# Other points in the pace at which a four-layer hybrid kernel streams its modulation weights

## The chip, the cores and the metric

The kernel runs on one core of a Trainium2 chip. The metric is device time in microseconds (us) of one execution, given as the median of several. A core has five engines that work side by side, each through its own instructions in order: TensorE (PE; its weight loads are listed as PEld), VectorE (DVE), ScalarE (ACT), GpSimd (POOL) and SyncE (SP). SP computes nothing here: it issues most of the transfers from memory, in order, and waits for the target buffer of each before it issues it.

## The reference

Four residual layers over 256 tokens of width 2048, batch 1, float32 throughout. Layer `i` first makes three vectors of 2048 from a conditioning vector `c`; the layer kinds are RWKV-7 (layers 0 and 3), gated linear attention (layer 1) and a state-space layer, SSD (layer 2).

```python
c_act = silu(c)
for i in range(4):
    mod = einsum('bd,de->be', c_act, ada_w[i]) + ada_b[i]     # ada_w[i]: 2048 x 6144
    shift, scale, gate = split(mod, 3)
    h = rms_normalize(x, norm_g[i]) * (1 + scale) + shift
    out = (rwkv7_mixer, gla_mixer, ssd_mixer)[i % 3](h, ...)  # projections in, a scan, a projection out
    x = x + gate * out
return rms_normalize(x, final_g)
```

Every `(i, q)` with `q` = 0, 1, 2 (shift, scale, gate) is called a **third** here: 2048 x 2048 weights against one vector. The reference does them ahead of each layer; none of them depends on `x`, so a kernel can do them at any time before they are used.

## The kernel before

**Projections.** `x` is kept as 16 tiles of 128 channels by 256 tokens. A projection takes its weights in **chunks** of up to 128 x 1024 float32 (512 KB). For each chunk, SP loads it into one of the six buffers `raw` (L348), ACT rounds it to `H` (L338), DVE makes the rest `L = raw - H` (L340), and PE multiplies `H` with both parts of the input and `L` with the first (L393). After the matmuls of each chunk, `jobs` (L359) calls `tick` (L395). There are 670 ticks; 36 further chunks (the first part of layer 0's V projection, and the small low-rank weights of layers 0 and 3) have none, so that L338 runs 706 times. Counted by these casts in time order, ticks can be laid over the trace: that is how the stretches of the tables below were cut.

**The stages, in ticks.** Layer 0 (RWKV): the end of V is 1 to 8, K 9 to 40, R 41 to 72, G 73 to 104, the output projection 105 to 144 (in three parts, of four, three and one of the eight head groups). While K is projected, `rwkv_first` works on DVE, ACT, PE and the transfers of SP and POOL for each of eight head groups; it ends in `unit_inverse`, a chain of small DVE steps and transfers through memory. `rwkv_second` does the scan during R and after. Layer 1 (GLA) is 145 to 276, layer 2 (SSD) 277 to 502, in eight groups of 20 ticks with an output projection of 16 ticks after each second group, and layer 3 (RWKV) 503 to 670.

**The thirds.** `ada_third` (L290) does one third in 32 **steps** of a generator: a step loads 512 KB of `ada_w` into a buffer `raw`, the same six as above, by SP (L298), and DVE adds it, multiplied by the entry of `c_act` for each row, to the running sum `adaacc` (L304; ACT does the first of 16, L302). After each 16 steps, eight matmuls of PE (L310, L316), a copy of ACT and an addition of DVE (L317) put the half third into `mod`. The shift and scale of layer 0 are done ahead, in another way, by `ada_group`. Ten thirds are left, in the order (0,2), (1,0), (1,1), (1,2), (2,0) ... (3,2): 320 steps and one that closes the last.

**The pace.** `tick` reads the number of steps due at this tick from `PACE` (L96): ticks and steps, with straight lines between. It takes at most two steps at one tick. It takes none while `hold` is set, which is from the last 256 columns of a layer's output projection until the first projection of the next layer is through. Whoever uses a third calls `ada_need` (L331), which takes all steps that are still missing at once: `norm_parts` (L498) and `scaled` need shift and scale at the start of a layer, and `outproj` (L424) the gate. Steps forced like this are not counted by `tick`, so the generator is ahead by as many from then on.

**The order.** A scheduler in the compiler lays out each engine's order from the order in which the program names the instructions, and moves an instruction forward where it expects its engine to be free. Steps that come after a layer's end in the program can so stand among the last instructions of the layer.

Of the kernel before, what the change touches and what calls it, by code (L numbers as in the profile page):

```python
# [92 lines left out]

RAWC = 1024

PACE = ((0, 60, 78, 150, 319, 530, 660), (0, 0, 16, 96, 234, 292, 320))  # L96

SHARE = (1, 0, 1, 0, 1, 0, 1, 0)

# [30 lines left out]
class Kern:  # L130
# [264 lines left out]
    def tick(self):  # L395

        self.tk += 1
        n = min(int(np.interp(self.tk, *PACE)), self.paced + 2)
        if not self.hold:
# [1072 lines left out]
```

## Time and profile before

| | us |
|---|---|
| median of 3 runs | 2889.27 |
| lowest and highest | 2874.83, 2891.78 |
| the profiled execution | 2887.0 |
| its span, from its first to its last instruction | 2885.0 |

The rows further down are from the profiled execution, whose own time is 2 us over its span and 2 us under the median. An engine's busy time is the union of its instructions; "(x12)" is a count. "PEclk" is TensorE's granted clock as a share of 2.4 GHz, so 0.50 is 1.2 GHz. In a timeline row the bracket at the end is the engine's idle time before the instruction, and what ended it.

### The profile page before, as it was taken

The page shows a single profiled execution, that of the slowest core. Times are in us where ns is not written, and L with a number is a line of the kernel's source. Part 1 is how long each engine was busy: PE and PEld are TensorE (multiplying, and loading weights), DVE is VectorE, ACT ScalarE, POOL GpSimd, SP SyncE. Part 2 cuts the span into 40 slices and gives each one's busy share as a digit, 9 for nine tenths or more (in the row PEclk, how much of TensorE's full clock was granted, in tenths as well). Part 3 has the DMA queues.
Part 4 walks back from the last instruction along what each step waited for, and adds up shares of the span by engine and source line. Part 5 has one row for each costly group of instructions (what it writes and reads, how often), then busy time and mean ns, then how long its engine had stood idle before and what let it go on. Part 6 is the DMA issues. An engine that isn't in the chain of part 4 may idle for free.

```text
span 2885.0 us, 64064 instructions
## 1 busy us (share of the span) xinstructions
PE 2686.2 (93%) x26098; PEld 2505.1 (87%) x26098; DVE 2212.4 (77%) x3918; ACT 1392.8 (48%) x2315; POOL 154.6 (5%) x298
## 2 busy tenths in 40 slices
PE   6899999999987899988998999999889999999997
PEld 4789889887877899987988999999879988988887
DVE  5778777877788888877898788887668897666666
ACT  3475655433335454434544454554457756453333
POOL 0011110101000000000000000000000111010100
PEclk8899999999998999999999999999989999999999
DMA  9866557977677888976784767776557665585543
GB/s 348 308 231 190 176 161 261 347 266 278 207 261 244 293 285 291 324 268 197 277 294 161 242 219 228 224 226 216 167 171 236 230 208 190 178 297 194 207 132 108
DMA packets 239126, 673.68 MB, mean 234 GB/s; under 512 B 72272, under 2 KB 78416, under 8 KB 235760
## 3 DMA queue, kind: packets, MB, share of 16 engines
q1 hardware_dynamic: 217904, 580.84, 60.2%
q0 software_dynamic: 20928, 88.75, 8.5%
q8 instruction: 205, 3.36, 0.5%
q14 instruction: 89, 0.73, 0.1%
HBM read 620.66 MB, written 48.82 MB: 232 GB/s over the span
## 4 chain that ended last, share of the span: by engine, by line
PE 66%; DVE 8%; DMA 8%; issue 3%; ACT 2%; SPq 1%; POOL 0%; DVEq 0%; ACTq 0%; POOLq 0%
PE acc L393 53%; DMA raw<-in_ada_w 3%; DVE L L340 2%; PE g L785 2%; DVE adaacc L304 1%; ACT H L338 1%; PE b L897 1%; DMA raw<-in_gla_w_in 1%; DMA dx<-bd 1%; DMA raw<-in_rwkv_w_in 1%; PE b L866 1%; DMA raw<-in_rwkv_w_out 1%; PE b L873 1%; DMA sp<-yd 1%; PE b L1030 1%
## 5 line engine op out<-in xcount | busy, mean ns | idle before, releaser
L393 PE MATMUL acc<-xs,H 128*128 128x256 f32 x8480 | 1634.4, 291 | 36.5 <-ACT H L338 8.1
L393 PEld LDWEIGHTS acc<-xs,H 128*128 128x128 f32 x8480 | 1362.8, 196 | 69.3 <-ACT H L338 11.4
L393 PE MATMUL acc<-xs,L 128*128 128x256 f32 x4240 | 1230.6, 291 | 17.1 <-DVE L L340 16.2
L338 ACT CAST H<-raw 128x1024 fp32r<-128x1024 f32 (+1 forms) x706 | 718.0, 1018 | 854.9 <-PE acc L393 634.3
L340 DVE TENSOR_TENSOR L<-raw,H 128x1024 fp32r<-128x1024 f32 (+1 forms) x706 | 833.7, 1183 | 248.9 <-ACT H L338 234.0
L393 PEld LDWEIGHTS acc<-xs,L 128*128 128x128 f32 x4240 | 830.8, 196 | 31.1 <-DVE L L340 21.5
L304 DVE SCALAR_TENSOR_TENSOR adaacc<-raw,cact,adaacc 128x1024 f32<-128x1024 f32 x300 | 384.0, 1280 | 132.6 <-DMA raw<-in_ada_w 130.2
L393 PE MATMUL acc<-ys,H 128*128 128x256 f32 x1536 | 293.3, 291 | 12.2 <-DVE ys L409 4.9
L393 PEld LDWEIGHTS acc<-ys,H 128*128 128x128 f32 x1536 | 245.9, 195 | 22.0 <-issue 6.6
L393 PE MATMUL acc<-ys,L 128*128 128x256 f32 x768 | 222.1, 290 | 0.4 <-DVE L L340 0.4
L393 PEld LDWEIGHTS acc<-ys,L 128*128 128x128 f32 x768 | 149.6, 195 | 4.6 <-issue 3.6
L551 ACT ACTIVATE hn<-x,mod,omu 128x256 f32<-128x256 f32 x192 | 113.4, 599 | 1.5 <-DVE x L542 1.2
L431 DVE SCALAR_TENSOR_TENSOR x<-acc,mod,x 128x256 f32<-128x256 f32 x192 | 83.6, 477 | 35.7 <-PE acc L393 35.3
L393 PE MATMUL acc<-H,xs 128*128 128x256 f32 x512 | 97.1, 290 | 1.6 <-ACT vt L1078 1.6
L554 DVE SCALAR_TENSOR_TENSOR xm<-x,par,hn 128x256 f32<-128x256 f32 x192 | 88.6, 476 | 1.4 <-ACT hn L551 0.3
L393 PEld LDWEIGHTS acc<-H,xs 128*128 128x128 f32 x512 | 82.4, 197 | 3.1 <-ACT vt L1078 1.8
L393 PE MATMUL acc<-L,xs 128*128 128x256 f32 x256 | 73.8, 289 | 0.0
L785 PE MATMUL g<-abkp 64*128 64x128 f32 x768 | 65.8, 293 | 4.0 <-DVE G L823 2.7
L408 ACT CAST xs<-xm 128x256 fp32r<-128x256 f32 x128 | 50.9, 400 | 35.4 <-DVE xm L554 33.0
L785 PEld LDWEIGHTS g<-abkp 64*128 64x128 f32 x768 | 52.2, 190 | 15.8 <-issue 8.8
L1284 DVE SCALAR_TENSOR_TENSOR cva<-cvp,hcw,cva 128x256 f32<-128x256 f32 x144 | 64.9, 476 | 0.0
L278 DVE SCALAR_TENSOR_TENSOR adaacc<-raw,cact,adaacc 128x512 f32<-128x512 f32 x56 | 41.9, 748 | 27.5 <-DMA raw<-in_ada_w 23.0
(358 smaller groups left out, 3063.0 us busy)
## 6 DMA issues: line engine op xcount, KB each, us to landing
raw<-in_ada_w SPq DMA_DIRECT2D x384, 512.0 KB, 4.8
raw<-in_rwkv_w_in SPq DMA_DIRECT2D x256, 512.0 KB, 4.7
raw<-in_ssd_w_in SPq DMA_DIRECT2D x128, 512.0 KB, 4.4
raw<-in_gla_w_in SPq DMA_DIRECT2D x96, 512.0 KB, 5.2
raw<-in_ssd_w_out SPq DMA_DIRECT2D x64, 512.0 KB, 4.2
raw<-in_rwkv_w_out SPq DMA_DIRECT2D x48, 512.0 KB, 4.2
abkp<-kd POOLq DMA_DIRECT2D x16, 1024.0 KB, 7.3
raw<-in_gla_w_out SPq DMA_DIRECT2D x32, 512.0 KB, 4.9
```

Of the source, the lines that this page charges most:

```text
L278: nc.vector.scalar_tensor_tensor(out=acc, in0=raw[:, u, :], scalar=self.cact[:, k:k + 1], in1=acc, op0=ALU.mult, op1=ALU.add)
L304: nc.vector.scalar_tensor_tensor(out=acc, in0=raw, scalar=self.cact[:, k:k + 1], in1=acc, op0=ALU.mult, op1=ALU.add)
L338: nc.scalar.copy(out=hi, in_=raw[:, a:a + n])
L340: nc.vector.tensor_tensor(out=lo, in0=raw[:, a:a + n], in1=hi, op=ALU.subtract)
L393: self.nc.tensor.matmul(ps, lhs, rhs, start=first and part == 0 and w is hi, stop=last and w is lo)
L408: nc.scalar.copy(out=t[:, 0, :], in_=src)
L431: nc.vector.scalar_tensor_tensor(out=self.x[:, t, 1:], in0=ps[:, u, :], scalar=gate[:, t:t + 1], in1=self.x[:, t, 1:], op0=ALU.mult, op1=A ...
L551: nc.scalar.activation(t1, x[:, k, 1:], AF.Identity, scale=self.omu[:, col:col + 1], bias=self.mods[(i, 0)][:, k:k + 1])
L554: done[k] = nc.vector.scalar_tensor_tensor(out=xm, in0=x[:, k, 0:T], scalar=self.p("rwkv_mu", col), in1=t1, op0=ALU.mult, op1=ALU.add)
L785: self.nc.tensor.matmul(ps[h][:, n * C:(n + 1) * C], s[r, q, c * C:(c + 1) * C], t[r, q, c * C:(c + 1) * C], start=True, stop=True)
L866: nc.tensor.matmul(ps[r, n * H:(n + 1) * H], G[h][:, q, r], tk[:, 2, q, HS[h]], start=not c, stop=not c or h == 1)
L1284: nc.vector.scalar_tensor_tensor(out=a, in0=src[:, k:k + T], scalar=w[k], in1=a, op0=ALU.mult, op1=ALU.add)
```

## The change

One line: the points of `PACE`. No instruction is added or taken away; the 320 steps, with their loads and sums, come at other ticks.

```diff
-PACE = ((0, 60, 78, 150, 319, 530, 660), (0, 0, 16, 96, 234, 292, 320))
+PACE = ((0, 57, 134, 272, 496, 620), (0, 36, 98, 194, 290, 320))
```

Worked through `tick`, `hold` and `ada_need` by hand, the two lists give these steps (times are those of the kernel before):

| stage | ticks | us of the span | steps before | steps after |
|---|---|---|---|---|
| layer 0, end of V | 1-8 | 180-201 | 0 | 5 |
| layer 0, K | 9-40 | 201-343 | 0 | 20 |
| layer 0, R | 41-72 | 343-498 | 10 | 23 |
| layer 0, G and output, first part | 73-120 | 498-784 | 52 | 38 |
| layer 0, output, other parts | 121-144 | 784-872 | 26 | 18 |
| forced at the start of layer 1 by (1,1) | | 872-890 | 9 | 0 |
| layer 1, decay and head 0 | 145-172 | 890-988 | 25 | 20 |
| layer 1, other heads, first output | 173-260 | 988-1272 | 72 | 61 |
| layer 1, last output | 261-276 | 1272-1345 | 12 | 9 |
| layer 2, groups 0, 1, first part of 2 | 277-330 | 1345-1549 | 40 | 24 |
| forced at the first output of layer 2 by (2,2) | | | 0 | 7 |
| layer 2, first output | 331-346 | 1549-1611 | 4 | 7 |
| layer 2, rest of group 2 to group 7 | 347-486 | 1611-2047 | 38 | 60 |
| layer 2, last output | 487-502 | 2047-2120 | 4 | 5 |
| layer 3 | 503-670 | 2120-2885 | 29 | 24 |

## Rows read from the trace of the kernel before

**Rows 1.** The page, engines: busy us, share of the span, instructions.
```profile
PE 2686.2 (93%) x26098; PEld 2505.1 (87%) x26098; DVE 2212.4 (77%) x3918; ACT 1392.8 (48%) x2315; POOL 154.6 (5%) x298
```

**Rows 2.** The page, costliest groups: busy, mean ns | idle before, releaser.
```profile
L338 ACT CAST H<-raw 128x1024 fp32r<-128x1024 f32 (+1 forms) x706 | 718.0, 1018 | 854.9 <-PE acc L393 634.3
...
L304 DVE SCALAR_TENSOR_TENSOR adaacc<-raw,cact,adaacc 128x1024 f32<-128x1024 f32 x300 | 384.0, 1280 | 132.6 <-DMA raw<-in_ada_w 130.2
```

**Rows 3.** Windows, all engines: stretch, us, busy by engine, PEclk, DMA share, GB/s.
```profile
201.00:343.00 142.00, 136.39 (x1508) 129.81 (x1506) 115.95 (x253) 90.84 (x178) 15.32 (x28) 0.98 0.59 188
343.00:498.00 155.00, 145.77 (x2128) 138.19 (x2129) 108.80 (x206) 84.05 (x158) 15.78 (x31) 0.92 0.64 203
498.00:784.00 286.00, 270.34 (x2900) 242.31 (x2899) 223.58 (x379) 100.76 (x164) 30.71 (x57) 0.95 0.80 278
784.00:872.00 88.00, 74.60 (x617) 64.51 (x615) 69.54 (x111) 30.36 (x54) 1.07 (x2) 0.96 0.74 257
...
890.00:988.00 98.00, 90.81 (x664) 83.69 (x665) 83.56 (x114) 55.72 (x86) 0.52 (x1) 0.93 0.71 245
988.00:1272.00 284.00, 282.38 (x2322) 269.07 (x2321) 230.28 (x287) 129.22 (x180) 0.00 (x0) 1.00 0.84 298
1272.00:1345.00 73.00, 64.98 (x467) 58.20 (x465) 51.22 (x73) 27.58 (x46) 0.00 (x0) 0.91 0.71 238
1345.00:1549.00 204.00, 181.46 (x1441) 172.68 (x1441) 180.13 (x335) 105.36 (x161) 2.72 (x5) 0.92 0.73 253
1549.00:1611.00 62.00, 55.09 (x449) 52.86 (x448) 47.23 (x92) 25.12 (x34) 0.53 (x1) 0.92 0.57 187
1611.00:2047.00 436.00, 435.63 (x3693) 428.00 (x3692) 357.15 (x633) 221.01 (x312) 1.59 (x3) 1.00 0.69 223
2047.00:2120.00 73.00, 64.21 (x472) 56.23 (x471) 40.81 (x70) 25.49 (x41) 4.34 (x6) 0.91 0.51 169
2243.00:2390.00 147.00, 137.17 (x1363) 129.51 (x1362) 123.32 (x263) 93.58 (x183) 14.92 (x26) 0.95 0.67 219
...
2538.00:2808.00 270.00, 267.00 (x3136) 241.19 (x3135) 175.80 (x337) 100.84 (x168) 31.79 (x59) 0.99 0.60 206
2808.00:2869.00 61.00, 60.13 (x509) 54.92 (x507) 40.74 (x80) 26.92 (x46) 0.00 (x0) 1.00 0.32 100
```

**Rows 4.** Windows of L304 alone: stretch, us, DVE busy (count), PEclk, DMA share, GB/s.
```profile
498.00:784.00 286.00, 61.49 (x48) 0.95 0.80 278
784.00:872.00 88.00, 30.73 (x25) 0.96 0.74 257
...
988.00:1272.00 284.00, 86.84 (x68) 1.00 0.84 298
...
1345.00:1549.00 204.00, 44.79 (x35) 0.92 0.73 253
...
1611.00:2047.00 436.00, 44.88 (x35) 1.00 0.69 223
...
2243.00:2390.00 147.00, 7.68 (x6) 0.95 0.67 219
...
2538.00:2808.00 270.00, 5.10 (x4) 0.99 0.60 206
```

**Rows 5.** Timeline of PE at the ends of layers 0 and 1.
```profile
872.34 0.61 PE L471 MATMUL nb<-cst,hn 128*128 128x1 f32 x4 [0.46 <-ACT hn L468]
882.97 1.08 PE L310 MATMUL mx<-adaacc,cst 128*32 128x256 f32 x8 [10.03 <-DVE rsr L1049]
...
889.83 0.58 PE L393 MATMUL b<-xs,H 128*128 128x256 f32 x1 [1.52 <-ACT xs L411]
...
1348.47 0.61 PE L471 MATMUL b<-cst,hn 128*128 128x1 f32 x4 [0.41 <-ACT hn L468]
...
1358.85 0.80 PE L393 MATMUL acc<-xs,H 128*128 128x256 f32 x2 [1.52 <-ACT xs L411]
```

**Rows 6.** Timeline of SP's issues at the end of layer 0.
```profile
862.42 11.14 SPq L298 DMA_DIRECT2D raw<-in_ada_w  x8
```

## The prediction, made before the run

> **What bounds the kernel now.** First comes the page's line of engines: PE is busy for 93% of the span, DVE for 77% [rows 1], so that the whole is near PE's work and no average tells what a step costs. I therefore read the windows, cut at the stages. Two regimes stand side by side. In the middle of layer 1 PE has no gap to speak of (282.4 of 284 us) though 68 steps' sums (L304) lie in it; in the later groups of layer 2 it is the same (435.6 of 436 us), with 35 of them [rows 3, 4]. There a step more or less is covered by PE. At the start of layer 2, though, DVE is busy for 180.1 of 204 us, 0.883, while PE has 23 us of gaps and a granted clock of 0.92 [rows 3]: what ends last there is DVE. I take **0.883** as the most that DVE reaches in a stretch of this kernel that it bounds. Last, the timeline at the layers' ends: at the end of layer 0, PE has done the norm's last small matmul at 872.3 and begins layer 1 at 889.8, 17.5 us later; at the end of layer 1 the same takes 10.4 us (1348.5 to 1358.9) [rows 5]. At the end of layer 0 SP issues eight loads of modulation weights one after another, in 11.1 us [rows 6]: these are the nine steps forced by the third (1,1), as counted in the table of the change. PE's long wait there ends with DVE's reciprocal root (L1049), which shares DVE with their sums.
>
> **The change, part by part.** Nothing is removed; each moved step takes along 512 KB on SP's queue and on the six buffers, and 1.28 us of DVE [rows 2]. Gains are negative; steps are those of the table.
>
> *Layer 0, K: 20 steps more.* DVE is busy for 115.95 of 142 us without one [rows 3]. With 20 x 1.28 = 25.6 us it would need 141.6 us; at 0.883 that takes 160 us, **+18**. Layer 3's K carries 6 sums and takes 147 us [rows 3, 4]: 5 us for 6, by which 20 cost 17. I take **+17**. Ends: 0 (141.6 fits in 142 if DVE had no gap) and +26 (each at its full length). The load that waits for a buffer has behind it on SP's queue the next chunk's load and the transfers of `unit_inverse`, for whose landing DVE waits: this is what could push it to the upper end. The Trainium skill (Perfetto Trace Analysis, section Identifying the Most-Contended Engine) would have us look for the engine with the highest occupancy and optimize it first; in K that is PE, with 136.4 against DVE's 116.0 us, and read so, K's term would be 0 and the sum 17 lower. The start of layer 2 speaks against leaning on the order of the two: there they are within 1.4 us of each other and both have gaps.
>
> *End of V, 5 more.* Layers 0 and 3 give a price for mild loads: G with the first part of the output takes 286 us with 48 sums and 270 us with 4, 16 / 44 = 0.36 us each [rows 3, 4]. For 5: **+2**; ends 0 and +6 (full length).
>
> *R, 13 more.* DVE has 108.8 of 155 us; with 16.6 more it is at 0.81 [rows 3], as in the middle of layer 1 where PE has no gaps. So the mild price, 13 x 0.36 = **+5**; ends 0 and +17.
>
> *G and first output, 14 fewer.* The same price, **-5**; ends 0 and -10 (twice that).
>
> *Output, other parts: 8 fewer.* This stage takes 88 us with 25 sums in layer 0 and 61 us with none in layer 3 [rows 3, 4], 27 / 25 = 1.08 us each: 8 x 1.08 = 9. By DVE: 40.74 us without sums, 18 x 1.28 = 23.0 more, over 0.883: 72 us, a gain of 16. I take **-11**, nearer to the measured price; ends -4 and -20.
>
> *The forced nine, gone.* The new pace has 104 steps there, seven over what (1,1) needs, so the end of layer 0 becomes like that of layer 1 now, where later steps also stand among the norm's instructions: 10.4 for 17.5, **-7**. Ends 0 and -10. What is late next is the norm's own chain of DVE, PE and ACT.
>
> *Layer 1.* Decay and head 0 have 5 steps fewer, in 98 us with DVE at 83.6, 0.85 [rows 3], near the ceiling. A sum there is worth up to 1.28 / 0.883 = 1.45 us, so at most 7; **-4**. The other heads lose 11 under a full PE: **0**. The last output has 3 fewer; it takes 73 us, and so does layer 2's last output, with next to no steps [rows 3]: **0**, at best -5.
>
> *Layer 2, start: 16 fewer.* DVE would need 180.1 - 20.5 = 159.6 us, at 0.883 181 us, a gain of 23. At K's price, 0.83 us each, it is 13. PE alone needs 181.5 us less what its clock cost it. I take **-15**, nearer to the measured price; ends -5 and -24.
>
> *Layer 2, first output: 3 more and 7 forced.* In the new pace, tick 330 has 218 steps and the gate (2,2) needs 225, so `ada_need` takes 7 at once ahead of the first output projection. Eight such loads held SP's queue for 11.1 us [rows 6]; queued behind these 7 are the output's own chunks, and on DVE the sums stand ahead of group 2's work. PE has the chunks already loaded, and may write two accumulators before it needs the gate. Nothing in the trace of before shows how much of this is covered, as the forced steps there met an empty PE. Ends: -5 (the stage, now 62 us, has gaps of 7 us [rows 3] that could close by a lighter DVE before it) and +14 (7/8 of 11.1, and 3 sums at 1.28). I take **+7**, half of the upper end.
>
> *Rest of layer 2: 22 more.* DVE goes from 357.2 to 385 of 436 us, which is 0.883 itself, under a PE without gaps. Ends 0 and +28. The middle of layer 1 has 0.24 sums per us at no cost; here they go from 0.08 (35 in 436) to 0.13 [rows 3, 4]; I take **+5**, below the mild price (8).
>
> *Last output of layer 2, and layer 3: 4 fewer in all, spread.* **0**, within 3 either way.
>
> Sum: 17 + 2 + 5 - 5 - 11 - 7 - 4 - 15 + 7 + 5 = -6, on 2887.0: 2881. The profiled execution lies 2 us under the median, so 2883 beside 2889.3; I give **2882**. The pace moves the price of DVE's sums from four places to four others, and little is left over. One per cent (29 us) is about what a measurement of this kernel can tell from no change.
>
> **Rivals.**
> *(A) Slower: K and R don't take more DVE work.* If the chains of `unit_inverse` and the scan set DVE's share there, added sums lengthen the stages at today's shares: K 141.6 / 0.817 = 173, +31; R 125.4 / 0.702 = 179, +24; V's end +9 (6.4 / 0.702). That is 64 instead of 24, the sum +34: **2921**. For: DVE waits for transfers of the inverse in K, and these share SP's queue. Against: layer 3's K has 0.84 with 6 sums. It is slower than before once V, K and R together cost over 30 us.
> *(B) Faster: sums are free where DVE has gaps and cost the ceiling's price where it has none.* K +7 (at 0.95), V, R and the rest of layer 2 at 0; the two relieved stages at their DVE figures, -16 and -23. Sum: 7 - 5 - 16 - 7 - 4 - 23 + 7 = -41: **2846**. For: full PE in layers 1 and 2 under 68 and 35 sums. Against: the measured 5 us for 6 sums in layer 3's K. The Trainium skill (Perfetto Trace Analysis, section Optimization Strategy) says that where the contended engine changes over time, interleaving the regimes may improve performance; that is this case, and no run here has shown it yet.
> *(C) The change doesn't do what it says:* the third (2,2) is not complete in time, and its forced steps cost what those of layer 0 did, a stop of 17.5 us instead of 7. Sum +4: **2891**. For: the count. Against: PE has work waiting there.
>
> **How the numbers follow.** The forecast has 0.50, A 0.15, B 0.22, C 0.13. The terms' ends, taken as independent, put some 28 us either way on the forecast, and B and A lie beyond; a range from **2850 to 2915** leaves out about half of A and B each. Faster by over 1% (under 2860): three quarters of B and a little of the forecast, 0.20. Slower by over 1% (over 2918): over half of A and a little of the forecast, 0.12. Within 1%: 0.68.
>
> **What would show it.** Right: K near 160 us with about 20 sums and DVE near 0.88; the stop at the end of layer 0 near 10 us; layer 2's start some 15 us shorter with about 19 sums; seven loads in a row on SP before layer 2's first output, with a gap of PE of some us behind them. Wrong: K at 173 or more (A), K under 150 and the later groups of layer 2 without gaps (B), PE standing for 15 us or more at the first output of layer 2 (C). The prediction fails as a whole if the compiler's new order opens gaps in places where the number of steps didn't change.

## The result, and the profile after

| | before | after |
|---|---|---|
| median | 2883.82 us (6 runs) | 2908.19 us (6 runs, 2900.42 to 2909.74) |
| ratio after / before | | 1.0081, 95% interval 1.0054 to 1.0107 |
| the profiled execution | 2887.0 us | 2903.33 us |
| its span | 2885.0 us | 2901.2 us |

The kernel became 24 us slower. The time lies inside the range of 2850 to 2915, but the forecast, 2882, had a small gain. The page of the changed kernel first: its engines, its chain that ended last (shares by engine) and its group of the sums, which answer to [rows 1, 2]. The row by itself below is the chain of the kernel before.

```profile
PE 2690.8 (93%) x26098; PEld 2505.2 (86%) x26098; DVE 2212.6 (76%) x3918; ACT 1396.8 (48%) x2315; POOL 154.3 (5%) x298
...
PE 59%; DMA 17%; DVE 15%; issue 5%; ACT 2%; SPq 1%; DVEq 0%; POOL 0%; ACTq 0%; POOLq 0%
...
L304 DVE SCALAR_TENSOR_TENSOR adaacc<-raw,cact,adaacc 128x1024 f32<-128x1024 f32 x300 | 384.2, 1281 | 228.7 <-DMA raw<-in_ada_w 224.8
```

```profile
PE 66%; DVE 8%; DMA 8%; issue 3%; ACT 2%; SPq 1%; POOL 0%; DVEq 0%; ACTq 0%; POOLq 0%
```

Every busy time is as it was. What has changed is the end of the sums' row: DVE stood idle 228.7 us ahead of them, against 132.6 [rows 2], nearly all of it for their own loads; and in the chain DMA and DVE have taken shares from PE. The windows tell where, against [rows 3, 4]; first all engines (us, busy by engine PE, PEld, DVE, ACT, POOL, PEclk, DMA share, GB/s), then the sums alone:

```profile
201.00:349.00 148.00, 137.48 (x1416) 129.73 (x1414) 129.67 (x252) 90.20 (x174) 14.61 (x26) 0.95 0.76 246
349.00:501.00 152.00, 144.79 (x1966) 135.90 (x1965) 125.12 (x234) 83.98 (x157) 16.34 (x33) 0.90 0.72 240
501.00:795.00 294.00, 272.03 (x3108) 244.80 (x3108) 212.40 (x360) 104.28 (x172) 30.64 (x57) 0.97 0.73 259
795.00:871.00 76.00, 69.09 (x615) 62.84 (x613) 59.77 (x111) 28.21 (x49) 1.06 (x2) 0.93 0.66 213
...
979.00:1266.00 287.00, 282.94 (x2322) 269.84 (x2321) 217.67 (x278) 127.75 (x177) 0.00 (x0) 1.00 0.81 278
...
1339.00:1527.00 188.00, 175.38 (x1440) 168.26 (x1438) 167.46 (x321) 103.16 (x158) 2.71 (x5) 0.96 0.68 239
1527.00:1595.00 68.00, 54.35 (x434) 51.44 (x435) 52.24 (x97) 25.92 (x36) 0.53 (x1) 0.90 0.62 211
1595.00:2063.00 468.00, 446.87 (x3703) 434.07 (x3702) 381.38 (x652) 223.54 (x313) 1.58 (x3) 0.99 0.69 232
```

```profile
501.00:795.00 294.00, 50.81 (x40) 0.97 0.73 259
...
979.00:1266.00 287.00, 75.67 (x59) 1.00 0.81 278
...
1595.00:2063.00 468.00, 71.85 (x56) 0.99 0.69 232
```

The stages cut at the same ticks in both traces (a tick by the start of its chunk's cast on ACT), in us, against the terms of the prediction:

| stage | before | after | change | predicted |
|---|---|---|---|---|
| layer 0: end of V | 20.9 | 24.4 | +3.5 | +2 |
| K | 142.0 | 147.9 | +5.9 | +17 |
| R | 154.8 | 152.7 | -2.1 | +5 |
| G and output, first part | 286.7 | 293.4 | +6.7 | -5 |
| output, other parts (with the stop at its end) | 94.2 | 75.8 | -18.4 | -11 - 7 |
| layer 1: decay and head 0 | 109.3 | 108.3 | -1.0 | -4 |
| other heads, first output, last output | 351.5 | 354.2 | +2.8 | 0 |
| layer 2: start, ticks 277-330 | 209.6 | 193.4 | -16.2 | -15 |
| first output, 331-346 | 62.3 | 68.6 | +6.3 | +7 |
| **rest, 347-486** | **436.1** | **467.8** | **+31.7** | **+5** |
| last output | 72.4 | 77.1 | +4.7 | 0 |
| layer 3 | 765.1 | 761.1 | -4.0 | 0 |

Up to tick 331 the changed kernel is ahead, 1526.6 us for 1549.1 (3.6 of it from ahead of tick 1). It loses that and more from there to the end of layer 2. In ticks 347 to 486 PE, which had 0.4 us of gaps, has 21 (468.00 - 446.87), while DVE's share has not risen with its 21 further sums: 381.38 / 468.00 = 0.815, for 357.15 / 436.00 = 0.819. The other 11 us of the loss are in PE's busy time itself (446.87 for 435.63). Its granted clock there was 0.99 for 1.00: it stood at 0.50, the level of 1.2 GHz, in three short stretches (below), 13.7 us in all, each at the end of a stop of PE of 2 to 4 us or right behind it. By these rows I estimate that at up to 7 of the 11 us, half of 13.7; so the loss here is more than the length of the stops.

```profile
1625.50:1628.90 3.40, 3.40 (x19) 3.40 (x18) 3.25 (x5) 1.70 (x4) 0.00 (x0) 0.50 0.90 323
1745.00:1751.80 6.80, 4.25 (x17) 3.51 (x18) 6.80 (x14) 1.47 (x4) 0.00 (x0) 0.50 0.35 107
1864.50:1867.90 3.40, 3.40 (x18) 3.40 (x17) 3.28 (x6) 0.92 (x2) 0.00 (x0) 0.50 0.72 220
```

What DVE waited for there (line, from whom: us in all, times, longest), before and after:

```profile
DVE adaacc L304 <- DMA raw<-in_ada_w: 33.9, 27, 2.7
DVE L L340 <- ACT H L338: 30.0, 31, 1.7
```

```profile
DVE adaacc L304 <- DMA raw<-in_ada_w: 70.4, 38, 5.0
DVE L L340 <- ACT H L338: 6.9, 9, 1.7
```

The waits at the sums are doubled, for 56 sums instead of 35. Busy time and these waits together fill (357.15 + 33.9) / 436 = 0.90 of the stretch before and (381.38 + 70.4) / 468 = 0.97 after. PE in turn waits for DVE's late L's, 0.4 us in all before; its waits in the same stretch, after:

```profile
PE acc L393 <- DVE L L340: 12.6, 13, 2.6
PE acc L393 <- ACT ys L408: 3.8, 1, 3.8
```

How one such wait looks is seen in the timelines of SP, of DVE and (one row) of ACT around the end of the first output of layer 2 after the change:

```profile
1577.21 0.33 SPq L298 DMA_DIRECT2D raw<-in_ada_w  x1
...
1585.06 0.33 SPq L298 DMA_DIRECT2D raw<-in_ada_w  x1
1586.98 4.57 SPq L348 DMA_DIRECT2D raw<-in_ssd_w_in  x2
1592.36 0.33 SPq L298 DMA_DIRECT2D raw<-in_ada_w  x1
```

```profile
1582.62 1.28 DVE L304 SCALAR_TENSOR_TENSOR adaacc<-raw,cact,adaacc 128x1024 f32<-128x1024 f32 x1 [2.52 <-DMA raw<-in_ada_w]
1583.82 1.22 DVE L340 TENSOR_TENSOR L<-raw,H 128x1024 fp32r<-128x1024 f32 x1
1584.95 0.87 DVE L431 SCALAR_TENSOR_TENSOR x<-acc,mod,x 128x256 f32<-128x256 f32 x2
1585.74 1.22 DVE L340 TENSOR_TENSOR L<-raw,H 128x1024 fp32r<-128x1024 f32 x1
1589.91 1.28 DVE L304 SCALAR_TENSOR_TENSOR adaacc<-raw,cact,adaacc 128x1024 f32<-128x1024 f32 x1 [2.96 <-DMA raw<-in_ada_w]
1591.12 1.22 DVE L340 TENSOR_TENSOR L<-raw,H 128x1024 fp32r<-128x1024 f32 x1
```

```profile
1586.38 1.05 ACT L338 CAST H<-raw 128x1024 fp32r<-128x1024 f32 x1 [1.83 <-PE acc L393]
```

The sum follows 4.9 us after its own load is issued (1585.06 to 1589.91); DVE stands 2.96 us for it, and makes two L's in 7.29 us (1582.62 to 1589.91). The `H` of the next L was ready at 1587.43 (1586.38 + 1.05), 2.5 us before the sum began. The Trainium skill (PSUM — Partial Sum Buffer, section Engine vs sequencer instructions) says that VectorE's queue is strictly first in, first out; the trace agrees, this L, at 1591.12, comes only behind the sum.

Where do the sums stand in DVE's order? I counted for each sum the chunks whose load SP issued before the sum's own load, and whose L DVE makes only after the sum. The count is 0 where a sum keeps its place behind the L's that the program names ahead of it. In the middle of layer 1 before it is mostly 1 (39 of 68 sums), in ticks 331-486 before it is 3 or 4 (40 of 40). After the change it is 2 or 3 in layer 1's middle (46 of 59) and 3 or 4 in ticks 331-486 (51 of 65). So the compiler had moved the sums forward on DVE, past the L's of several chunks. In layer 1's middle all waits at sums came to 7.6 us before (68 sums) and to 48.3 after (59), at a loss of 3.6 us under a full PE; in layer 2 the waits had been there from the start, but hidden.

### The profile page after: what moved, and what is told of

It reads as the page before. It is cut to its first block, busy times and chain, and to the rows that moved or that the text cites. A ratio compares the mean times of both kernels' runs of the same rounds, so it can differ in the third digit from the quotient of the medians.

```text
span 2901.2 us, 64001 instructions
## 1 busy us (share of the span) xinstructions
PE 2690.8 (93%) x26098; PEld 2505.2 (86%) x26098; DVE 2212.6 (76%) x3918; ACT 1396.8 (48%) x2315; POOL 154.3 (5%) x298
## 4 chain that ended last, share of the span: by engine, by line
PE 59%; DMA 17%; DVE 15%; issue 5%; ACT 2%; SPq 1%; DVEq 0%; POOL 0%; ACTq 0%; POOLq 0%
PE acc L393 46%; DMA raw<-in_ada_w 12%; DVE L L340 5%; DVE adaacc L304 2%; PE pv L393 2%; PE g L785 2%; ACT H L338 1%; DMA raw<-in_rwkv_w_in 1%; DMA dx<-bd 1%; PE b L897 1%; DMA xd<-dx 1%; DVE dt L958 1%; DMA sp<-yd 1%; DMA bd<-LT 1%; PE b L866 1%
## 5 line engine op out<-in xcount | busy, mean ns | idle before, releaser
L304 DVE SCALAR_TENSOR_TENSOR adaacc<-raw,cact,adaacc 128x1024 f32<-128x1024 f32 x300 | 384.2, 1281 | 228.7 <-DMA raw<-in_ada_w 224.8
```

What stands on the lines that cost most here:

```text
L304: nc.vector.scalar_tensor_tensor(out=acc, in0=raw, scalar=self.cact[:, k:k + 1], in1=acc, op0=ALU.mult, op1=ALU.add)
```

## The experiments

All were timed in five rounds beside the kernel before on the same chip; ratios are to that. "The order" below is an order on DVE without a wait. Where expectations use letters, W is the theory that DVE's waits at the sums make the loss, D that DVE's work does (the ceiling that the prediction used elsewhere), F that the forced steps of (2,2) do (the prediction's rival C), O that the loss is spread over the whole, and B that buffers held longer, or bytes, delay the chunks. The first two kernels take the change apart by layers.

**e1_layer0: the new points in layer 0, the old pace behind it.**

```diff
-PACE = ((0, 57, 134, 272, 496, 620), (0, 36, 98, 194, 290, 320))
+PACE = ((0, 57, 134, 144, 319, 530, 660), (0, 36, 98, 105, 243, 301, 329))
```

> The new pace up to tick 144 (layer 0), then a pace that gives layers 1 to 3 nearly the steps of the kernel before (246 at tick 330, 288 at tick 486). Theory W (in layer 2 DVE stands at sums whose loads have not landed, and the chunks queue behind them) and theory D (DVE has too much work there) both put the loss in layer 2 and a gain of 0 to 8 us in layer 0, by the stages of the two traces: 2876 to 2884, ratio to before 0.997 to 1.000. Theory O (the loss is spread, from the compiler's other order of everything): about half of the loss, 1.004.

2907.98 us, ratio 1.0095 (1.0075 to 1.0115): a miss for all three theories. Ticks 331-486 took 494 us as before (498), but layer 1's other heads took 304 us (66 sums, 56 us of waits at them, 14 us of gaps in PE) against 284. Its profiled execution, 2916.29 us, was its slowest, and layer 0, which is the same program as in the changed kernel, ended 14 us later in it (884.6 for 870.6). So a single stage in one profile is good to some us only, and layer 1 can be hurt by the waits as well.

**e2_layers12: the old pace in layer 0, the new slopes from layer 1 on.**

```diff
-PACE = ((0, 57, 134, 272, 496, 620), (0, 36, 98, 194, 290, 320))
+PACE = ((0, 60, 78, 144, 272, 496, 620), (0, 0, 16, 89, 185, 281, 311))
```

> The other part alone: the pace of before up to tick 143 with the forced steps at the end of layer 0, then the new slopes (219 steps at tick 330, 6 forced by the gate of layer 2, 292 at tick 486). W and D: the whole loss of the change and more, since the gain of layer 0 is missing: 2908 to 2916, ratio 1.008 to 1.011. O: about 1.004.

2936.97 us, ratio 1.0200 (1.0176 to 1.0225), another miss for all, though ticks 347-486 took 471 us as in the changed kernel (468). Here too layer 1's other heads took longer, 305 us (64 sums, 58 us of waits). In the changed kernel 48 us of such waits had gone with a loss of 3.6 us in that stage; 56 to 58 go with 20 to 21. Against the kernel before (2879.61 us on this chip) the parts give +28 and +57, the whole +24: points can't be priced one by one.

**e3_cut: the sums without their loads' landing.** The sums of (3,0) and (3,1) read resident constants in place of their loads. (The constant `kmask` was also moved to the end of the constants, out of the part that is read; that part of the edit isn't shown.)

```diff
+                    src = self.cst[:, 0:RAWC] if i == 3 and q < 2 else raw
-                    nc.vector.scalar_tensor_tensor(out=acc, in0=raw, scalar=self.cact[:, k:k + 1], in1=acc,
+                    nc.vector.scalar_tensor_tensor(out=acc, in0=src, scalar=self.cact[:, k:k + 1], in1=acc,
```

> The new pace; the sums of the thirds (3,0) and (3,1), steps 225 to 288, which are most of those in the later part of layer 2, read a resident tile of constants in place of the weights that are loaded; the loads go on, unread, so that DVE's work and the bytes are the same and only the wait of a sum for its load is gone (layer 3's shift and scale are then wrong). W: the 32 us lost in ticks 331 to 486 come back but for the forced steps, 2878 to 2886. D: nothing changes, 2905 to 2911.

2907.71 us, ratio 1.0099 (1.0079 to 1.0119): the time that D expected, and not W. But the sums, free of the wait, were also laid out elsewhere: 16 of them in the first output, the sixth group's output 64 us for 53; and layer 3's K and R took 314.5 us for 295.8. So the whole decides nothing. Ticks 331-486 took 519 us (536), and 347-486 of them 452 with 49 sums and next to no wait.

**e4_later: the load a step earlier than its sum.**

```diff
                 nc.sync.dma_start(out=raw, in_=self.A["ada_w"][3 * i + q - 2, g, k])
+                yield
                 if k == 0:
-                    yield
...
-                if 0 < k < DT - 1:
-                    yield
...
-            yield
```

> The new pace; in each step of a third the load is issued, and its sum follows one step later (at least a tick, most often two or three), so that the data has landed when DVE comes to the sum; loads, sums and bytes are the same, and one of the six buffers is held by a waiting load at all times. W: DVE's 225 us of waits for these loads fall below 60 and the 32 us of ticks 331 to 486 come back, 2870 to 2884. D: nothing changes, 2905 to 2911. A rival, B: the held buffer delays the chunks, 2915 to 2930.

2911.04 us, ratio 1.0107 (1.0087 to 1.0127), close to D's time again. But the edit didn't take the waits away, and so tests neither theory: 61.7 us of them are left in ticks 347-486, with a median of 5.2 us from a load's issue to its sum in ticks 331-486. Naming a sum later doesn't make it late; the compiler moved it forward again.

**e6_order: each sum ordered on DVE behind the last L ahead of it in the program.** No wait on another engine is added; the compiler only may not move the sum forward past that L. Lines behind L304 have a number one higher in this kernel.

```diff
-                    nc.vector.scalar_tensor_tensor(out=acc, in0=raw, scalar=self.cact[:, k:k + 1], in1=acc,
-                                                   op0=ALU.mult, op1=ALU.add)
+                    op = nc.vector.scalar_tensor_tensor(out=acc, in0=raw, scalar=self.cact[:, k:k + 1], in1=acc,
+                                                        op0=ALU.mult, op1=ALU.add)
+                    self.after(op, self.rest)
...
-        nc.vector.tensor_tensor(out=lo, in0=raw[:, a:a + n], in1=hi, op=ALU.subtract)
+        self.rest = nc.vector.tensor_tensor(out=lo, in0=raw[:, a:a + n], in1=hi, op=ALU.subtract)
```

> The new pace; each sum of a third must stand on DVE behind the L of the last chunk that the program named before it (an order on one engine, no wait). In the traces of before and after, sums of layer 2 stand 3 or 4 chunks ahead of that place, right behind the landing that the compiler expected, and DVE waits about 1 us at each. Work, loads and bytes are the same. W (DVE's waits at the sums are the loss): waits under 50 us in all, ticks 331 to 486 back to some 505 us from 536, total 2870 to 2885. D (work): 2905 to 2911. B (a buffer is held until the sum's late place, and the chunks' loads run less far ahead): slower, 2915 to 2935.

**2859.48 us, ratio 0.9918 (0.9888 to 0.9947)**: the loss is gone, and more than W expected. The count above is 0 for all 64 sums in ticks 331-486. Its windows of the outputs of groups 4 and 6, and then of the whole of ticks 347-486:

```profile
1711.00:1770.00 59.00, 54.76 (x446) 52.68 (x445) 50.08 (x93) 25.29 (x34) 0.53 (x1) 0.94 0.65 215
1897.00:1953.00 56.00, 53.44 (x449) 51.93 (x449) 48.75 (x86) 24.64 (x34) 0.00 (x0) 0.97 0.63 210
1584.00:2036.00 452.00, 441.28 (x3702) 432.28 (x3701) 381.34 (x651) 220.94 (x312) 1.59 (x3) 0.99 0.71 240
```

The same 381 us of DVE work and 56 sums now take 452 us for 468, so that DVE's share is 0.844 for 0.815. The timeline of DVE at the same place as above: two L's and a sum in 5.72 us (1566.57 to 1572.29), without a wait at the sum.

```profile
1566.57 1.28 DVE L304 SCALAR_TENSOR_TENSOR adaacc<-raw,cact,adaacc 128x1024 f32<-128x1024 f32 x1
1567.77 0.87 DVE L432 SCALAR_TENSOR_TENSOR x<-acc,mod,x 128x256 f32<-128x256 f32 x2
1568.56 1.21 DVE L341 TENSOR_TENSOR L<-raw,H 128x1024 fp32r<-128x1024 f32 x1
1571.14 1.23 DVE L341 TENSOR_TENSOR L<-raw,H 128x1024 fp32r<-128x1024 f32 x1 [1.37 <-ACT H L339]
1572.29 1.28 DVE L304 SCALAR_TENSOR_TENSOR adaacc<-raw,cact,adaacc 128x1024 f32<-128x1024 f32 x1
```

**e8_order_before: e6_order's order with the old pace.** As an edit of e6_order:

```diff
-PACE = ((0, 57, 134, 272, 496, 620), (0, 36, 98, 194, 290, 320))
+PACE = ((0, 60, 78, 150, 319, 530, 660), (0, 0, 16, 96, 234, 292, 320))
```

> The same order of the sums in the kernel before, with its pace. W: little, since its layer 2 has no gaps of PE; 130 us of DVE's waits fall, layer 0 may gain some: 2865 to 2882. B: slower, 2890 or more.

2868.49 us, ratio 0.9958 (0.9941 to 0.9976). Without the waits the new pace is the better one: 2859.48 to 2868.49, 9 us, where with them it is 24 us worse. Five of e6_order's six runs lie below the lowest of e8_order_before's twelve (2864.29); their profiled executions, 2864.17 and 2864.68, don't show the difference, so that its place among the stages is open. Ticks 347-486 took 439.6 us with 36 sums.

**e7_noforce: (2,2) complete before its gate, so that nothing is forced.**

```diff
-PACE = ((0, 57, 134, 272, 496, 620), (0, 36, 98, 194, 290, 320))
+PACE = ((0, 57, 134, 272, 330, 496, 620), (0, 36, 98, 194, 226, 290, 320))
```

> The new pace with one point more, (330, 226): the gate of layer 2 is complete at its first use and nothing is forced; eight steps more in the start of layer 2, and the slope after it (0.39 a tick for 0.43) gives 60 steps in ticks 331 to 486 for 74. W: the forced steps are no special cause; fewer sums with waits, the start of layer 2 dearer: 2900 to 2908. F (the forced steps are what cost ticks 331 to 354 some 14 us): 2890 to 2897.

2936.09 us, ratio 1.0182 (1.0154 to 1.0210), slower than either theory expected. The first output took 64.8 us for 68.6, but ticks 347-486 473.7, with 76 us of waits at sums, and layer 3's K and R 316.0 for 295.8, with 32 us of such waits for 8. The forced steps are not the cause of the loss; F falls.

**e5_gla: 32 steps more by the end of layer 1.**

```diff
-PACE = ((0, 57, 134, 272, 496, 620), (0, 36, 98, 194, 290, 320))
+PACE = ((0, 57, 134, 276, 496, 620), (0, 36, 98, 226, 290, 320))
```

> The new pace in layer 0, then 120 steps in layer 1 for 90 (226 at tick 276) and 46 in ticks 331 to 486 for 74 (before: 42). Under W layer 1's steeper pace puts the sums further back in DVE's order, with few waits and no cost, and layer 2 is as before: 2872 to 2884. D: DVE in layer 1 would be at 0.88 and pay some 15 us there: 2890 to 2900.

2895.08 us, ratio 1.0046 (1.0027 to 1.0066): D's time, but not for D's reason, a loss in layer 1. Layer 1's other heads took 77 sums at 289.3 us (287.3 with 59), the first output of layer 2 52.2 us and ticks 347-486 443.1, with 41.6 us of waits. Layer 3's K and R lost 19 us (315.2), with 36 us of waits.

**e9_short: e6_order's order, and the sums of (3,0) and (3,1) cut to 16 of their 1024 columns.** As an edit of e6_order:

```diff
-                    op = nc.vector.scalar_tensor_tensor(out=acc, in0=raw, scalar=self.cact[:, k:k + 1], in1=acc,
-                                                        op0=ALU.mult, op1=ALU.add)
+                    n = 16 if i == 3 and q < 2 else RAWC
+                    op = nc.vector.scalar_tensor_tensor(out=acc[:, 0:n], in0=raw[:, 0:n], scalar=self.cact[:, k:k + 1],
+                                                        in1=acc[:, 0:n], op0=ALU.mult, op1=ALU.add)
```

> e6 (the new pace, each sum behind its place in DVE's order), and the sums of the thirds (3,0) and (3,1), most of those in the later part of layer 2, add 16 of 1024 columns; each still reads its own loaded buffer at the same place, so that loads, bytes and the time for which a buffer is held are the same (layer 3's shift and scale are then wrong). Ticks 347 to 486 take 436 us in before, 468 in after, 452 in e6. D (what e6 leaves is DVE's work): 436 to 441 there, total 2843 to 2849. B (what it leaves is buffers and bytes): 448 to 455, total 2855 to 2864.

2842.07 us, ratio 0.9848 (0.9825 to 0.9872). The loads stay, and most of DVE's work for those 60 sums is gone: one takes 0.23 us for 1.28. Its windows of the same stretches as in e6_order:

```profile
1701.00:1752.00 51.00, 51.00 (x444) 49.76 (x443) 40.07 (x80) 23.01 (x28) 0.53 (x1) 1.00 0.71 252
1878.00:1929.00 51.00, 51.00 (x444) 49.76 (x443) 38.41 (x75) 23.12 (x27) 0.00 (x0) 1.00 0.65 231
1577.00:2013.00 436.00, 436.00 (x3700) 428.02 (x3699) 332.09 (x653) 219.06 (x314) 1.58 (x3) 1.00 0.71 248
```

PE is full at 436 us, the 436.1 of before, with DVE's work down from 381.34 to 332.09 us. The loads, their bytes and their buffers are all there, so that B falls too. That divides the 31.7 us, in this order of taking them off: 468 to 452 is the waits, 452 to 436 DVE's work. And of the 16 of work some 13 lie in the two outputs (59 + 56 - 2 x 51), where DVE is at 0.85 and 0.87 with seven sums each.

**e11_order_l2 and e12_order_l01: the order for the sums from (2,2) on alone, and for those up to (2,1) alone.**

As an edit of e6_order, the first of the two (the second has `< 8`):

```diff
-                    self.after(op, self.rest)
+                    if 3 * i + q >= 8:
+                        self.after(op, self.rest)
```

> The changed pace, with each sum of the thirds (2,2) and later ordered behind the last L ahead of it in the program; from tick 272 on these are all sums, those of layers 0 and 1 stay as in the changed kernel. If the waits at the sums cost their time where they stand, layers 0 and 1 take what they took in the changed kernel (tick 277 near 1333 us), and from there to the end the kernel takes what the wholly ordered one took (1542 us against 1568): 2882 us, from 2872 to 2892, with ticks 347-486 near 452 us and next to no wait at their sums. The rival is that the order gained by another arrangement of the whole and not by these waits: then layer 2 keeps ticks 347-486 over 460 us though its waits are gone, and the kernel takes 2895 us or more.

2878.86 us, ratio 0.9994 (0.9975 to 1.0013). Windows of ticks 347-486:

```profile
1594.00:2045.00 451.00, 440.05 (x3701) 430.78 (x3700) 381.36 (x651) 220.46 (x313) 1.59 (x3) 0.99 0.71 240
```

> The other half: the order for the sums of the thirds up to (2,1) alone, that is in layers 0 and 1. If the waits cost where they stand, tick 277 begins near 1320 us as in the wholly ordered kernel (1333 in the changed one) and layer 2 keeps its waits: ticks 347-486 near 468 us with some 70 us of waits at their sums, in all 2895 us, from 2885 to 2905. By the rival (another arrangement of the whole) the two halves don't add up to the 49 us of the wholly ordered kernel, and ticks 347-486 change here too.

2896.40 us, ratio 1.0045 (1.0024 to 1.0065). Windows and DVE's waits of the same ticks:

```profile
1577.00:2050.00 473.00, 446.24 (x3704) 432.55 (x3703) 380.92 (x652) 223.31 (x314) 1.58 (x3) 0.99 0.68 229
```

```profile
DVE adaacc L304 <- DMA raw<-in_ada_w: 75.8, 43, 4.8
```

Both came out as the theory of the waits had it: 451 us where the order holds, 473 where it doesn't. From the changed kernel's ratio of 1.0081 the order takes 0.9% off for the sums from (2,2) on, 0.4% off for those ahead of it, and 1.6% off in the whole. The halves fall 0.4% short of the whole, which the four intervals (0.2 to 0.3% either way each) leave open to chance.

**e10_gla_order: e6_order's order with e5_gla's pace (and its last point a step higher).** As an edit of e6_order:

```diff
-PACE = ((0, 57, 134, 272, 496, 620), (0, 36, 98, 194, 290, 320))
+PACE = ((0, 57, 134, 276, 496, 620), (0, 36, 98, 226, 290, 321))
```

> e6's order with the pace of e5 (226 steps by tick 276, 46 in ticks 331 to 486). D and W together: layer 1 still covered by PE, the first output of layer 2 near 52 us for 65 and ticks 347 to 486 near 440 for 452, the start of layer 2 some 8 us shorter with 17 sums for 27; layer 1's head 0, with more sums, up to 10 us longer: 2830 to 2848. If layer 1 can't take 120 steps: 2855 to 2870.

**2833.58 us, ratio 0.9814 (0.9789 to 0.9839)**: it beats both kernels. Windows of layer 1's ticks 173-260, and of ticks 331-346 and 347-486:

```profile
983.00:1268.00 285.00, 281.74 (x2320) 268.65 (x2319) 236.83 (x296) 129.18 (x180) 0.00 (x0) 1.00 0.87 312
1523.00:1575.00 52.00, 51.84 (x447) 50.34 (x447) 45.79 (x81) 24.95 (x34) 0.53 (x1) 1.00 0.64 223
1575.00:2013.00 438.00, 435.99 (x3684) 428.10 (x3684) 362.38 (x635) 219.91 (x311) 1.58 (x3) 1.00 0.68 225
```

## Why the prediction was wrong

**The step that failed is "Rest of layer 2: 22 more"**, +5 against a measured 31.7, 3.7 us over its upper end too. Three things were wrong in it.

First, its price. I took the middle of layer 1 as proof that 0.24 sums per us cost nothing under a full PE. But the two places were not alike: before the change the sums there stood one chunk ahead and waited 7.6 us in all, while in layer 2 they stood three or four chunks ahead and already waited 33.9 us for 35 sums. That row was in the trace of before, in the waits of this stretch. I read a PE without gaps [rows 3] as cover for more, when it showed only that the cover hadn't run out.

Second, the upper end. Each further sum was bounded by its own 1.28 us, 22 x 1.28 = 28. A sum can also stop DVE until its load lands, 2 to 3 us in the rows above. e6_order against the changed kernel puts this at about 16 us of the stage, and e11_order_l2 and e12_order_l01 show that it goes where the order holds and stays where it doesn't.

Third, the work itself. I took DVE at 385 of 436 us, "0.883 itself", and so at the edge of free. It cost 16 us, as e9_short against e6_order shows, and mostly in the two output stretches: they had 4 and 5 sums and DVE at 0.90 and 0.87 before the change, at my ceiling already while PE was full. Windows of the outputs of groups 4 and 6, before:

```profile
1735.00:1787.00 52.00, 52.00 (x450) 50.71 (x450) 46.94 (x83) 25.08 (x34) 0.53 (x1) 1.00 0.69 228
1911.00:1963.00 52.00, 51.63 (x445) 50.15 (x444) 45.07 (x82) 24.70 (x33) 0.00 (x0) 1.00 0.68 210
```

An average over unlike stretches hid that some of them were full.

**Layer 0.** K with R came to +4 for a predicted +22. K's DVE rose by 129.67 - 115.95 = 13.7 us, not by the 25.6 of 20 sums; the number of its DVE instructions stayed, 252 for 253 [rows 3]. So 21 other instructions had gone out of K, while R's rose from 206 to 234 with 8 more sums: work that is not due can slide into the next stage, and the two had to be priced together. The ceiling held as such (129.67 / 148 = 0.88). Rival A, on K at 173, falls. G with the first output lost 6.7 instead of winning 5. Under the order it takes 260.8 us, but R takes 179.7 for 152.7 there: work changes places between these stages, so that only their sum tells something. Ticks 9 to 144 take 657.0 us in e6_order and 652.9 in e12_order_l01, for 669.8 in the changed kernel and 668.4 in e11_order_l2, which has no order there. So the order, which takes the waits at sums away there too, gains some 11 to 17 us in layer 0 as well; in which of its stages isn't shown.

**The end of layer 0** gave 18.4 for 11 + 7, with some luck in the sum: PE's stop there is 6.3 us now, 17.5 before [rows 5], 11 less for a predicted 7, and the output ahead of it (784.4 to 872.3 before, 794.8 to 877.8 after) 5 less for a predicted 11. No row of eight loads stands ahead of the stop. PE's timeline after:

```profile
877.75 0.61 PE L471 MATMUL nb<-cst,hn 128*128 128x1 f32 x4 [0.46 <-ACT hn L468]
881.39 1.16 PE L483 MATMUL nb<-xm,cst 128*128 128x256 f32 x2 [3.03 <-DVE xm L480]
884.07 0.58 PE L393 MATMUL b<-xs,H 128*128 128x256 f32 x1 [1.52 <-ACT xs L411]
```

**Layer 2 up to tick 346** was right in size, -16.2 for -15 and +6.3 for +7, and in its reason in part. DVE stayed at the ceiling in the start (167.46 / 188 = 0.89, and 0.88 before [rows 3]), but 11 sums left that stage (35 to 24), not those of 16 steps. Of the first output, the forced loads are there, answering to [rows 6], in SP's timeline; a stop of PE of 9.5 us follows (1537.9 to 1547.3), which ends with work of DVE for the next group (L1299):

```profile
1509.68 10.22 SPq L298 DMA_DIRECT2D raw<-in_ada_w  x6
```

```profile
1547.32 1.22 PE L483 MATMUL b<-xm,cst 128*128 128x256 f32 x2 [9.47 <-DVE cvp L1299]
```

Rival C, with 15 us or more, falls. In e7_noforce, where nothing is forced, the longest stop of PE in that output is 2.7 us, and 4 us of the stage come back, so that the forced steps were worth some 4 of the 6.3. Rival B, sums free where DVE has gaps, had its first sign (K under 150), but falls by its second, which did not come (21 us of gaps in the later groups of layer 2), and by e9_short: the sums cost 16 us in a stretch where DVE has gaps on average.

In the profiled executions the change was +16.3 us for a predicted -6, 22.3 apart: 26.7 come from the rest of layer 2 and 4.7 from its last output; the stages up to tick 346 (-12.5 for -11), layer 3 (-4.0) and what lies ahead of tick 1 (-3.6) take 9.1 off again. With the waits gone the new pace is worth 9 us, near the 6 of the sum. So the sum had the balance of DVE's work about right, but by luck in part, as errors in layer 0 cancel (K with R 18 us too dear, G with the first output 12 too cheap), and it had no term for where the sums stand in DVE's queue. Its last sentence named the compiler's order as what could break it, but looked for that where the number of steps stays.

The Trainium skill (DMA: Bandwidth & Descriptors, section Rules for kernel authors) says to issue a transfer early and to wait for it late. The runs agree: the later place of the sums alone was worth 1.6%; in ticks 331-486 the median from a load's issue to its sum went from 4.7 us to 11.4. To name the sum later in the program, as in e4_later, didn't do it.

What stays open: why the last output of layer 2 takes 4.7 us more, and why the compiler moves the sums further ahead at one pace than at another. That it expects a load to land sooner than the 4 to 5 us seen here was argued from the order, and not tried. How much of layer 0's and layer 1's smaller differences is the run rather than the pace can't be told from one profile each.

## What to carry to other kernels

Before pricing more background work under a full engine, read the waits of the engine that does it, not its busy share alone: busy time and the waits at that very work together came to 0.90 of the stretch before, without a loss, and to 0.97 with one. (That their sum can forecast a loss was not tried.) A consumer of a background transfer belongs in an in-order queue behind the foreground work that doesn't depend on it, by an explicit order if a compiler lays out the queue. With it, the new pace's gain in the whole, 9 us, came near that of the count of work, 6, though single stages of layer 0 did not. And cut a long window where its stages differ, since the ceiling is met in the fullest of them first.

## What the runs showed that I had not expected

An order that adds no instruction and no wait, only a later place of 300 sums of 1.28 us, was worth 1.6% (ratios 1.0081 and 0.9918). The same change of the pace cost 24 us without that order and gained 9 us with it. DVE's share of the stretch that lost most did not rise with 21 sums more (0.819 to 0.815), and rose to 0.844 when the waits went and the stretch became shorter: an engine that waits at the head of its queue doesn't look busier. And DVE's work that isn't due moved out of K by 21 instructions when 20 sums came in, with no change to its lines.
